# A 31-tap causal convolution summed in a PSUM bank, by halves of the tokens

## The chip, the cores and the metric

The kernel runs on one core of a Trainium2 chip. The metric is the device time of one execution in microseconds (us); a difference is told from the median of several runs. The engines are named as in the profile: PE is TensorE with its matmuls (PEld its weight loads), DVE is VectorE, ACT is ScalarE, POOL is GpSimd, and SP is the engine that issues the transfers. SBUF is the working memory, PSUM the memory that matmuls write: eight banks, each of which holds 512 float32 columns on every partition.

## The reference

One layer of a decoder over 1024 tokens of width 1024, batch 1. A normed and modulated input `h` is projected once; the columns go to four token mixers, whose outputs are joined and projected again, and a gated feed-forward block follows.

```
h = rmsnorm(x, ln1_g) * (1 + sc1) + sh1
a_val, a_gate, b_q, b_k, b_v, b_g, b_lr, c_q, c_k, c_v, d_u, d_v = split(h @ w_in)
o_a = silu(layernorm(causal_dwconv(a_val * sigmoid(a_gate), conv_w, conv_b)))   # CONV_K = 31, 256 channels
o_b = gla_mixer(b_q, b_k, b_v, b_g, b_lr, ...)      # gates from b_lr @ gla_w2
o_c = dilated_attention(c_q, c_k, c_v, cos, sin)    # rotary, masked scores, softmax
o_d = sgu_mixer(d_u, d_v, ...)
x = x + g1 * (concat(o_a, o_b, o_c, o_d) @ w_out)
x = x + g2 * conv_ffn(rmsnorm(x, ln2_g) * (1 + sc2) + sh2, ...)
out = rmsnorm(x, lnf_g)
```

The causal convolution works on each of the 256 channels by itself: y[s] = bias + the sum over j = 0..30 of w[30 - j] * h[s - j], with zeros ahead of the first token.

## The kernel before

The convolution has its channels on partitions and the tokens in columns: two tiles (`t` = 0, 1) of 128 channels and 1024 tokens. `hA[t]` holds the gated input, `yA[t]` the sum, both in SBUF. The generator `conv_taps` issues one DVE operation for each tap: L461 multiplies by the last weight and adds the bias, and L464 runs 30 times over the rest, each of which adds a shifted product to `yA[t]` in place: it reads `hA[t]` and `yA[t]` in SBUF and writes `yA[t]`. That makes 62 operations of nearly 1024 columns.

The rest of the mixers is woven around it. Every part of the work is a generator. `weave` runs a main one (projections on PE) and after each of its steps takes as many steps from the others as their rate allows; `conv` has the rate 2.74, 1.87 and 1.39 taps a step in the three stages that it spans. A framework then fixes the order on every engine, allots the buffers of its pools and adds the waits. Each engine works through its own queue strictly in order.

```
    weave(chain(proj_feat(gate1, (1,))), (conv, 2.74))
    weave(chain(proj_feat(rope("q0")), proj_feat(rope("k0")), proj_tok(c_v), proj_feat(rope("q1")), proj_feat(rope("k1"))),
          (conv, 1.87))
```

The names that the prediction uses: `p_s()` gives one of eight PSUM banks (tile `s_ps`), which the projections, scores and transposes share. Four gates (L454 sigmoid on ACT, L456 product on DVE) make `hA`. The projections of the attention (q0, k0, c_v, q1, k1) end in copies on ACT (L593 for q and k); for q and k four transfers on SP then swap halves of 32 partitions (L597, L598), and POOL does the rotation in three operations (L601 to L603). Weights are split into two parts, a cast on ACT (L70) and a difference on POOL (L71). In the next stage the projection `proj_glr` runs over eight token tiles; of each result DVE copies 16 columns into `lrs` (L752), and PE transposes them (L755). Beside it the attention starts: PE's scores (L92 to L94, `m_t,x_t`), DVE's masked maximum (L659, which reads the mask that L631 loads), ACT's exponential (L667), the quotient on DVE (L670), POOL (L672) and ACT, and transposes on PE (L695). L828 is a matmul of the modulation, which DVE adds up (L830).

Of the kernel before, what the change touches and what calls it, by code (L numbers as in the profile page):

```python
# [7 lines left out]
F32 = mybir.dt.float32  # L8
# [3 lines left out]
ALU = mybir.AluOpType  # L12
AX = mybir.AxisListType

P = 128
D = 1024
S = 1024
KT = D // P
# [3 lines left out]
CONV_K = 31  # L22
# [3 lines left out]

# feature tiles of the first modulation, in the order of their loads
ADA_1 = ((0,), (1,), (2, 3), (4, 5), (6, 7))

# first columns of the parts of w_in  # L30
C_AV, C_AG = 0, 256
# [5 lines left out]

# columns of the packed per-feature vectors
O_C, O_L1, O_L2, O_CG, O_CB, O_VB, O_GB, O_SB, O_AB = 0, 8, 16, 24, 26, 28, 30, 31, 35
O_CW = 83  # L40
# [6 lines left out]
def trunk(ctx, tc, x, cols, ada_1, ada_2, ada_b, w_a, w_feat, w_tok, w_glr, gla_w2, gla_norm_g,  # L47
# [3 lines left out]
    ve, ac, gp, pe, sy = nc.vector, nc.scalar, nc.gpsimd, nc.tensor, nc.sync  # L51


    cst = ctx.enter_context(tc.tile_pool(name="cst", bufs=1))
# [18 lines left out]
    def rsqrt(dst, ss, shape, scale, pool):  # L73
        # bit-level first guess, three Newton steps
        v = pool.tile(shape, F32, tag="rs_v", name="rs_v", bufs=2)
        t = pool.tile(shape, F32, tag="rs_t", name="rs_t", bufs=2)
        ve.tensor_scalar(v, ss, scale, EPS, op0=ALU.mult, op1=ALU.add)
        ve.tensor_scalar(dst.bitcast(I32), v.bitcast(I32), -0.5, 1597463007.0, op0=ALU.mult, op1=ALU.add)
        for _ in range(3):
            ve.tensor_tensor(t, dst, dst, op=ALU.mult)  # L80
            ve.scalar_tensor_tensor(t, t, -0.5, v, op0=ALU.mult, op1=ALU.mult)
            ve.scalar_tensor_tensor(dst, t, 1.5, dst, op0=ALU.add, op1=ALU.mult)
# [15 lines left out]

    # ---------------------------------------------------------------- constants
    ident = cst.tile([P, P], F32, name="ident")  # L100
# [6 lines left out]
    def cc(o, n=1):  # L107
        return col[:, o:o + n]
# [4 lines left out]
    adab1 = cst.tile([P, 2, KT], F32, name="adab1")  # L113
    mod = cst.tile([P, 5, KT], F32, name="mod")      # scale and shift of the first norm, of the second norm, gate of the feed-forward block

    # ---------------------------------------------------------------- emission: streams woven into one order
    active = []
# [9 lines left out]
    def weave(main, *bgs):  # L127
        credit = [0.0] * len(bgs)
        for _ in main:
            for n, (g, rate) in enumerate(bgs):  # L130
                credit[n] += rate
                while credit[n] >= 1:
                    credit[n] -= 1
                    next(g, 0)
            step()
# [8 lines left out]
    class Weights:  # L144
        """Weight tiles in the order of their use: loaded two ahead, split one ahead."""

# [33 lines left out]

    # ---------------------------------------------------------------- mixers
    ph1 = ExitStack()
# [8 lines left out]
    def p_s():  # L191
        return ps1.tile([P, 512], F32, tag="s", name="s_ps", bufs=8)
# [3 lines left out]

    # first norm: statistics, transposes
    g1b = c1.tile([P, 1024], F32, name="g1b")
# [3 lines left out]
    PM = (4, 0, 0, 0, 0)  # L202
# [12 lines left out]

    # the first PM[p] products of a group on TensorE, the others on VectorE
    def ada_mac(p):
# [70 lines left out]

    # modulation of the first norm and the first projections, feature tile by feature tile
    hH = [[None, None] for _ in range(KT)]  # L290
# [88 lines left out]

    # ---------------------------------------------------------------- projections  # L380
    def proj_feat(done, halves=(0, 1)):
        wh, wl = W1.get()
        for g in halves:
            ps = p_s()
            for k in range(KT):
                ks = slice(k * P, (k + 1) * P)
                mm3(ps, wh[:, ks], wl[:, ks], hH[k][g], hL[k][g], k == 0, k == KT - 1)
                if k == 3:
                    yield 1
            if g == 1:  # L390
                spawn(W1.refill())
            spawn(done(g, ps))
            yield 1
# [46 lines left out]
    def chain(*gens):  # L440
        for g in gens:
            yield from g

    have = set()                                     # what of oT is there, by (tile, half of the tokens)
    oT = [None] * 8                                  # feature-major outputs of the mixers, by tiles of 128 features
    oH = [[None, None] for _ in range(8)]
    oL = [[None, None] for _ in range(8)]

    # ---------------------------------------------------------------- A: gate, convolution, norm
    hA = [t_m(), t_m()]  # L450
# [7 lines left out]
    def conv_taps():  # L458
        for t in range(2):
            y = yA[t]  # L460
            ve.tensor_scalar(y, hA[t], cc(O_CW + 60 + t), cc(O_VB + t), op0=ALU.mult, op1=ALU.add)  # L461
            yield 1
            for s in range(1, CONV_K):
                ve.scalar_tensor_tensor(y[:, s:], hA[t][:, :S - s], cc(O_CW + (CONV_K - 1 - s) * 2 + t), y[:, s:], op0=ALU.mult, op1=ALU.add)  # L464
                yield 1

    def conv_norm():
# [44 lines left out]

    # ---------------------------------------------------------------- D: spatial gating
    dk = t_m()
# [63 lines left out]

    # ---------------------------------------------------------------- C: rotary
    cosT, sinT = t_m(), t_m()  # L580
# [35 lines left out]

    # first stage: the rest of A's and all of D's and C's projections, the convolution beside them
    conv = conv_taps()

    def gate1(g, ps):  # L620
# [3 lines left out]
    step()  # L624
    weave(chain(proj_feat(gate1, (1,))), (conv, 2.74))
    weave(chain(proj_feat(rope("q0")), proj_feat(rope("k0")), proj_tok(c_v), proj_feat(rope("q1")), proj_feat(rope("k1"))),
          (conv, 1.87))

    # ---------------------------------------------------------------- C: attention
    maskT = t_m()  # L630
# [87 lines left out]

    # ---------------------------------------------------------------- B: gates
    ngb = c1.tile([P, 64], F32, name="ngb")  # L720
# [83 lines left out]

    # ---------------------------------------------------------------- modulation of the rest
    ada_flat = ada_b.rearrange("a b -> (a b)")
# [42 lines left out]

    # second stage: B's projections, attention beside them  # L850
    att = attention([(hp, qb) for hp in range(2) for qb in range(NT)])
    weave(chain(proj_glr(), proj_tok(b_v), proj_feat(b_q), proj_feat(b_k)), (conv, 1.39), (att, 0.83), (ada, 2.06))
    flush(conv)
    cn = conv_norm()

    # ---------------------------------------------------------------- B: gated linear attention
    def split_o(kt, g):
# [107 lines left out]

    # third stage: D's projections, the rest of the attention and the linear attention beside them
    def delay(n, g):
# [17 lines left out]

    # ---------------------------------------------------------------- output projection, second norm, by halves of the tokens
    x1 = [None] * NT
# [77 lines left out]

    # ---------------------------------------------------------------- feed-forward block
    ph2 = ctx.enter_context(tc.tile_pool(name="ph2", bufs=1, reuse_waits="tile"))
# [94 lines left out]

    # last norm, by token tiles
    rows = {}

    def final(i, nh):
        if nh == 0:
            rows[i] = t_y(), ph2.tile([P, 4], F32, tag="ssf", name="ssf", bufs=2)
        t, ss = rows[i]
        cs = half(nh)  # L1170
        ac.activation(t[:, cs], x1[i][:, cs], AF.Square, accum_out=ss[:, 0:1])  # L1171
        ve.tensor_scalar(ss[:, nh + 1:nh + 2], ss[:, 0:1], 1.0 / D, ss[:, 1:2] if nh else EPS, op0=ALU.mult, op1=ALU.add)  # L1172
        gp.tensor_tensor(x1[i][:, cs], x1[i][:, cs], lnf[:, cs], op=ALU.mult)
        if nh == 1:
            # each Newton step multiplies by -2 (and the powers of it that the last one left), which lnf takes back
            v, w, u = ss[:, 2:3], rr[:, i:i + 1], ss[:, 3:4]
            ve.tensor_scalar(w.bitcast(I32), v.bitcast(I32), -0.5, 1597463007.0, op0=ALU.mult, op1=ALU.add)  # L1177
            for c in (1.0, -2.0, 16.0):
                ve.scalar_tensor_tensor(u, w, v, w, op0=ALU.mult, op1=ALU.mult)  # L1179
                ve.scalar_tensor_tensor(w, u, 3.0 * c * c, w, op0=ALU.subtract, op1=ALU.mult)  # L1180
            ac.mul(t[:, half(1)], x1[i][:, half(1)], w)  # L1181
            ve.tensor_scalar(t[:, half(0)], x1[i][:, half(0)], w, None, op0=ALU.mult)  # L1182
            sy.dma_start(out[i * P:(i + 1) * P, :], t)
# [86 lines left out]
```

## Time and profile before

| what | value |
|---|---|
| median of 3 runs | 1289.31 us (1288.96 to 1294.81) |
| span of the profiled execution, first to last instruction | 1287.0 us |
| median of the runs less that span | 2.3 us |
| busy: PE, DVE, POOL, ACT | 94%, 58%, 38%, 30% of the span |
| mean granted clock of PE | 0.978 |

The page gives the profiled execution by its span; its whole time is not listed apart from the runs, so the span is set beside their median. The mixers take the first 540 us or so, the feed-forward block the rest. Busy shares are means over all stages: where an engine matters is read from stretches of the span and from what each engine waits for.

### The profile page before, as it was taken

How to read it: one execution, taken by the hardware profiler on the slowest of the kernel's cores; microseconds unless marked ns; L12 is line 12 of the kernel's file. 1: busy time of each engine (PE TensorE's matmuls, PEld its weight loads, DVE VectorE, ACT ScalarE, POOL GpSimd, SP SyncE). 2: the span in 40 equal slices, each digit the busy share in tenths (PEclk: the TensorE clock that was granted, in tenths of full speed). 3: DMA queues.
4: the chain of work that ended last, by engine and by line, in shares of the span. 5: the costliest groups of instructions: out<-in, count | busy, mean ns of one | idle time of the engine just before them, and what ended most of it. 6: DMA issues, size and time to landing. Idle time of an engine off the chain costs nothing. (4 is left out here: it accounts for less than half of the span.)

```text
span 1287.0 us, 15986 instructions
## 1 busy us (share of the span) xinstructions
PE 1206.2 (94%) x6466; PEld 1013.9 (79%) x6466; DVE 746.1 (58%) x1193; ACT 390.8 (30%) x553; POOL 486.1 (38%) x260
## 2 busy tenths in 40 slices
PE   5899928999998999999999999999999999999995
PEld 4679817866797899978888888888888888888884
DVE  6989999576697965463534342425343434343467
ACT  5541205464331523343131313131212121212323
POOL 2557833322232466655141414131323232322424
PEclk9999968999998999999999999999999999999998
DMA  8632310222332532302020212121202021212102
GB/s 322 241 109 68 94 40 21 71 79 78 99 108 71 197 110 83 115 19 86 28 80 19 67 33 66 33 66 33 66 33 66 33 66 33 66 33 62 36 17 115
DMA packets 32842, 98.50 MB, mean 77 GB/s; under 512 B 3952, under 2 KB 5120, under 8 KB 32768
## 3 DMA queue, kind: packets, MB, share of 16 engines
q1 hardware_dynamic: 32768, 97.48, 23.3%
q8 instruction: 51, 0.84, 0.3%
q14 instruction: 23, 0.19, 0.0%
HBM read 91.17 MB, written 4.19 MB: 74 GB/s over the span
## 5 line engine op out<-in xcount | busy, mean ns | idle before, releaser
L71 POOL TENSOR_TENSOR wh_t<-wf_t,wh_t 128x1024 fp32r<-128x1024 f32 (+1 forms) x79 | 196.9, 2494 | 305.0 <-ACT wh_t L70 296.3
L92 PE MATMUL z_ps<-h_t,wh_t 128*128 128x512 f32 x704 | 274.4, 390 | 0.7 <-DVE y_t L1089 0.7
L93 PE MATMUL z_ps<-h_t,wh_t 128*128 128x512 f32 x704 | 274.8, 390 | 0.2 <-POOL h_t L71 0.2
L94 PE MATMUL z_ps<-h_t,wh_t 128*128 128x512 f32 x704 | 274.4, 390 | 0.0
L1089 DVE SCALAR_TENSOR_TENSOR y_t<-z_ps,col,y_t 128x1023 f32<-128x1023 f32 x88 | 112.5, 1280 | 227.8 <-ACT y_t L1086 226.7
L1157 DVE TENSOR_TENSOR x_t<-d_ps,x_t 128x512 f32<-128x512 f32 x170 | 116.7, 688 | 165.7 <-PE d_ps L94 165.7
L70 ACT CAST wh_t<-wf_t 128x1024 fp32r<-128x1024 f32 (+1 forms) x81 | 85.1, 1050 | 296.5 <-PE z_ps L92 136.9
L92 PEld LDWEIGHTS z_ps<-h_t,wh_t 128*128 128x128 f32 x704 | 132.2, 188 | 28.8 <-POOL wh_t L71 0.8
L93 PEld LDWEIGHTS z_ps<-h_t,wh_t 128*128 128x128 f32 x704 | 132.2, 188 | 28.5 <-POOL h_t L71 0.6
L94 PEld LDWEIGHTS z_ps<-h_t,wh_t 128*128 128x128 f32 x704 | 132.2, 188 | 27.4
L94 PE MATMUL d_ps<-wd_t,p_t 128*128 128x512 f32 x320 | 125.5, 393 | 0.0
L92 PE MATMUL d_ps<-wd_t,p_t 128*128 128x512 f32 x320 | 125.2, 391 | 0.0
L93 PE MATMUL d_ps<-wd_t,p_t 128*128 128x512 f32 x320 | 125.0, 391 | 0.0
L464 DVE SCALAR_TENSOR_TENSOR m_t<-m_t,col 128x1023 f32<-128x1023 f32 (+29 forms) x60 | 116.3, 1939 | 1.7
L71 POOL TENSOR_TENSOR wd_t<-wf_t,wd_t 128x1024 fp32r<-128x1024 f32 x20 | 47.7, 2403 | 160.2 <-ACT wd_t L70 160.2
L92 PE MATMUL s_ps<-wh_t,h_t 128*128 128x256 f32 (+1 forms) x320 | 93.7, 296 | 0.0
L93 PE MATMUL s_ps<-wh_t,h_t 128*128 128x256 f32 (+1 forms) x320 | 91.7, 287 | 0.9 <-POOL wh_t L71 0.9
L94 PE MATMUL s_ps<-wh_t,h_t 128*128 128x256 f32 (+1 forms) x320 | 91.7, 287 | 0.0
L1140 POOL TENSOR_TENSOR wf_t<-wf_t,g2b 128x1024 f32<-128x1024 f32 x22 | 53.9, 2449 | 77.1 <-DMA wf_t<-in_ffn_down 76.4
L821 DVE SCALAR_TENSOR_TENSOR acc<-ad,cond,acc 128x256 f32<-128x256 f32 x112 | 74.1, 665 | 12.4 <-DMA ad<-in_ada 10.5
L93 PEld LDWEIGHTS d_ps<-wd_t,p_t 128*128 128x128 f32 x320 | 60.2, 188 | 13.4
L92 PEld LDWEIGHTS d_ps<-wd_t,p_t 128*128 128x128 f32 x320 | 60.1, 188 | 13.3
(252 smaller groups left out, 2115.8 us busy)
## 6 DMA issues: line engine op xcount, KB each, us to landing
wf_t<-in_ffn_up SPq DMA_DIRECT2D x44, 512.0 KB, 3.6
ad<-in_ada SPq DMA_DIRECT2D x64, 256.0 KB, 3.4
wf_t<-in_ffn_down SPq DMA_DIRECT2D x22, 512.0 KB, 3.6
x_t<-in_x SPq DMA_DIRECT2D x16, 512.0 KB, 6.3
wf_t<-in_w_out SPq DMA_DIRECT2D x16, 512.0 KB, 3.7
m_t<-in_ada SPq DMA_DIRECT2D x12, 512.0 KB, 9.5
wf_t<-in_w_tok SPq DMA_DIRECT2D x8, 512.0 KB, 3.6
out<-y_t SPq DMA_DIRECT2D x8, 512.0 KB, 2.6
```

What stands on the lines that cost most here:

```text
L70: ac.copy(dst_h, src)
L71: eng.tensor_tensor(dst_l, src, dst_h.bitcast(F32), op=ALU.subtract)
L92: pe.matmul(ps, ll, rh, start=first, stop=False)
L93: pe.matmul(ps, lh, rl, start=False, stop=False)
L94: return pe.matmul(ps, lh, rh, start=False, stop=last)
L464: ve.scalar_tensor_tensor(y[:, s:], hA[t][:, :S - s], cc(O_CW + (CONV_K - 1 - s) * 2 + t), y[:, s:], op0=ALU.mult, op1=ALU.add)
L821: ve.scalar_tensor_tensor(acc, f[:, kk, :], cond[:, k:k + 1], acc, op0=ALU.mult, op1=ALU.add)
L1089: ve.scalar_tensor_tensor(y[:, s:e], z[:, s - n:e - n], cc(O_FW + 88 - 44 * n + f), y[:, s:e], op0=ALU.mult, op1=ALU.add)
L1140: gp.tensor_tensor(w[:, :1024], w[:, :1024], g2b, op=ALU.mult)
L1157: ve.tensor_tensor(x1[i][:, cs], pd, x1[i][:, cs], op=ALU.add)
```

## The change

`conv_taps` goes through each tile in two halves of 512 tokens. A half gets a PSUM bank `y` from `p_s()`. The first operation writes the last weight's product and the bias into it, and the next 29 add to it in place; they read `hA[t]` in SBUF and `y` in PSUM and write `y`. The last tap reads `y` and writes its half of `yA[t]` in SBUF. The first half has no input for the first `s` tokens of tap `s`, so it works on columns `s` to 511, and the last tap's 30 first columns go to `yA[t]` by a copy on ACT (L469). That makes 124 operations of up to 512 columns and two copies; the rates at which they are woven in are about doubled. Comments are also taken out, which moves nothing.

```
     def conv_taps():
         for t in range(2):
-            y = yA[t]
-            ve.tensor_scalar(y, hA[t], cc(O_CW + 60 + t), cc(O_VB + t), op0=ALU.mult, op1=ALU.add)
-            yield 1
-            for s in range(1, CONV_K):
-                ve.scalar_tensor_tensor(y[:, s:], hA[t][:, :S - s], cc(O_CW + (CONV_K - 1 - s) * 2 + t), y[:, s:], op0=ALU.mult, op1=ALU.add)
+            h = hA[t]
+            for g in range(2):
+                y, o, e = p_s(), 512 * g, 512 * g + 512
+                ve.tensor_scalar(y, h[:, o:e], cc(O_CW + 60 + t), cc(O_VB + t), op0=ALU.mult, op1=ALU.add)
                 yield 1
+                for s in range(1, CONV_K):
+                    a = 0 if g else s
+                    last = s == CONV_K - 1
+                    if last and a:
+                        ac.copy(yA[t][:, o:o + a], y[:, :a])
+                    ve.scalar_tensor_tensor(yA[t][:, o + a:e] if last else y[:, a:], h[:, o + a - s:e - s],
+                                            cc(O_CW + (CONV_K - 1 - s) * 2 + t), y[:, a:], op0=ALU.mult, op1=ALU.add)
+                    yield 1
...
-    weave(chain(proj_feat(gate1, (1,))), (conv, 2.74))
+    weave(chain(proj_feat(gate1, (1,))), (conv, 3.9))
     weave(chain(proj_feat(rope("q0")), proj_feat(rope("k0")), proj_tok(c_v), proj_feat(rope("q1")), proj_feat(rope("k1"))),
-          (conv, 1.87))
+          (conv, 3.8))
...
-    weave(chain(proj_glr(), proj_tok(b_v), proj_feat(b_q), proj_feat(b_k)), (conv, 1.39), (att, 0.83), (ada, 2.06))
+    weave(chain(proj_glr(), proj_tok(b_v), proj_feat(b_q), proj_feat(b_k)), (conv, 2.8), (att, 0.83), (ada, 2.06))
```

In the changed kernel the taps are L470 and each line behind them has a number higher by 7 (L752 is L759 there, L659 is L666). The text uses the numbers of before for all that both kernels have. PE's and POOL's orders are the same in both, apart from these numbers.

DVE, around the first `lrs`. `s_ps` and `m_t` with `col` are the convolution, `mx` is the score's maximum, and the brackets name the engines that a row waits for. Before, 55 operations of the convolution stand ahead of the first `lrs`:

```order
L464 SCALAR_TENSOR_TENSOR m_t<-m_t,col 128x1004 [waits DVE_49]
L659 ISA m_t,mx<-s_ps,m_t 128x128 [waits DMAHW3_49,DMAHW4_49,DMAHW2_49,DMAHW5_49,PE_49,DMAHW6_49,Activation_49,Pool_49]
L659 ISA mx 128x1
L464 SCALAR_TENSOR_TENSOR m_t<-m_t,col 128x1003 [waits DVE_49]
L663 TENSOR_SCALAR mx<-mx 128x1 [waits DVE_49]
L464 SCALAR_TENSOR_TENSOR m_t<-m_t,col 128x1002 [waits DVE_49]
L830 TENSOR_TENSOR g1b<-s_ps,adb 128x256 [waits PE_49]
L670 RECIPROCAL den<-den 128x1 [waits Activation_49]
L464 SCALAR_TENSOR_TENSOR m_t<-m_t,col 128x1001 [waits DVE_49]
L752 COPY lrs<-s_ps 128x16 [waits Activation_49]
```

In the changed kernel the same place has 108 halves ahead of it, and the first of these rows is the last tap of the first half of tile 1, which waits for ACT's copy:

```order
L470 SCALAR_TENSOR_TENSOR m_t<-m_t,col,s_ps 128x482 [waits Activation_49,Pool_49]
L470 SCALAR_TENSOR_TENSOR s_ps<-m_t,col,s_ps 128x512 [waits DVE_49] x4
L837 TENSOR_TENSOR g1b<-s_ps,adb 128x256 [waits DMAHW2_49,PE_49]
L470 SCALAR_TENSOR_TENSOR s_ps<-m_t,col,s_ps 128x512 [waits DVE_49]
L666 ISA m_t,mx<-s_ps,m_t 128x128 [waits DMAHW4_49,DMAHW3_49,DMAHW5_49,DMAHW2_49,Pool_49]
L666 ISA mx 128x1
L470 SCALAR_TENSOR_TENSOR s_ps<-m_t,col,s_ps 128x512 [waits DVE_49]
L759 COPY lrs<-s_ps 128x16 [waits Activation_49]
```

Ahead of `lrs` stand the same kinds of work, with L830 now ahead of L659 and L670 behind `lrs`. 16 halves are left behind the first `lrs`, where 7 taps were.

ACT, where the first rotary results are copied (`m_t<-s_ps` of 512 columns is such a copy). The changed kernel's order has the new copy of 30 columns between two of them, behind the cast of the rotated q0, which waits for POOL:

```order
L70 CAST m_t<-x_t 128x1024 [waits DMAHW6_49,DMAHW5_49,DMAHW7_49,DMAHW0_49,Pool_49]
L600 COPY m_t<-s_ps 128x512
L469 COPY m_t<-s_ps 128x30 [waits DVE_49]
L600 COPY m_t<-s_ps 128x512 [waits PE_49]
L70 CAST wh_t<-wf_t 128x1024 [waits DMAHW1_49,PE_49,Activation_49]
```

Before, the two copies follow each other directly. The second L469, of tile 1, stands behind the last of these copies (k1) and ahead of the copies of `proj_glr`.

SP, at the swaps of k1 (`x_t<-m_t`) and the load of the mask (`in_dil_mask`). Before:

```order
L154 DMA wf_t<-in_w_tok 128x1024 [waits DMAHW7_49,DMAHW5_49,Pool_49]
L631 DMA m_t<-in_dil_mask 128x1024
L597 DMA x_t<-m_t 32x1024 [waits Activation_49]
L598 DMA x_t<-m_t 32x1024 [waits DMAHW0_49]
L597 DMA x_t<-m_t 32x1024 [waits DMAHW1_49]
L598 DMA x_t<-m_t 32x1024 [waits DMAHW2_49]
```

In the changed kernel:

```order
L154 DMA wf_t<-in_w_tok 128x1024 [waits DMAHW7_49,DMAHW5_49,Pool_49]
L604 DMA x_t<-m_t 32x1024 [waits Activation_49]
L605 DMA x_t<-m_t 32x1024
L604 DMA x_t<-m_t 32x1024 [waits DMAHW0_49]
L605 DMA x_t<-m_t 32x1024 [waits DMAHW1_49]
L638 DMA m_t<-in_dil_mask 128x1024 [waits DMAHW2_49]
```

The mask has moved behind the four swaps, the first of which waits for ACT's copy of k1.

## Rows read from the trace of the kernel before

**Rows 1.** The page: busy time by engine, and the group of the taps.

```profile
PE 1206.2 (94%) x6466; PEld 1013.9 (79%) x6466; DVE 746.1 (58%) x1193; ACT 390.8 (30%) x553; POOL 486.1 (38%) x260
...
L464 DVE SCALAR_TENSOR_TENSOR m_t<-m_t,col 128x1023 f32<-128x1023 f32 (+29 forms) x60 | 116.3, 1939 | 1.7
```

**Rows 2.** What PE waited for: in total, times, longest.

```profile
PE s_ps L755 <- DVE lrs L752: 30.3, 1, 30.3
```

**Rows 3.** Stretches of 5 us: PE, PEld, DVE, ACT, POOL busy, clock, DMA.

```profile
170.00:175.00 5.00, 0.00 (x0) 0.00 (x0) 4.89 (x4) 0.00 (x0) 0.94 (x1) 0.63 0.00 0
...
200.00:205.00 5.00, 5.00 (x24) 4.78 (x23) 5.00 (x10) 0.00 (x0) 2.48 (x1) 0.50 0.00 0
205.00:210.00 5.00, 5.00 (x40) 4.29 (x38) 5.00 (x16) 4.20 (x9) 1.17 (x2) 0.96 0.00 0
```

**Rows 4.** Timeline of PE: start, length, instruction, and idle time before it.

```profile
140.63 0.39 PE L92 MATMUL s_ps<-h_t,wh_t 128*128 128x512 f32 x1
...
162.87 0.59 PE L828 MATMUL s_ps<-acc,ones 128*128 128x256 f32 x2
164.39 0.39 PE L93 MATMUL s_ps<-wh_t,h_t 128*128 128x272 f32 x1 [0.92 <-POOL wh_t L71]
...
199.07 0.38 PE L755 MATMUL s_ps<-ident,lrs 128*16 128x128 f32 x1 [30.28 <-DVE lrs L752]
...
205.71 0.27 PE L755 MATMUL s_ps<-ident,lrs 128*16 128x128 f32 x1
...
209.78 0.27 PE L755 MATMUL s_ps<-ident,lrs 128*16 128x128 f32 x1
```

**Rows 5.** Timeline of DVE, equal instructions merged.

```profile
92.35 66.85 DVE L464 SCALAR_TENSOR_TENSOR m_t<-m_t,col 128x1020 f32<-128x1020 f32 x27
...
162.01 32.25 DVE L464 SCALAR_TENSOR_TENSOR m_t<-m_t,col 128x1023 f32<-128x1023 f32 x20
194.18 0.28 DVE L659 CUSTOM_DVE_ANT_0 m_t<-s_ps,m_t 128x128 f32<-128x128 f32 x1
...
198.85 0.17 DVE L752 COPY lrs<-s_ps 128x16 f32<-128x16 f32 x1
```

**Rows 6.** Two stretches, all engines; then L464 from 105 to 140 (min/median/max).

```profile
106.00:136.00 30.00, 30.00 (x224) 28.80 (x223) 29.65 (x11) 4.12 (x5) 28.26 (x9) 1.00 0.27 74
...
171.00:194.00 23.00, 0.00 (x0) 0.00 (x0) 22.40 (x18) 0.00 (x0) 0.00 (x0) 0.51 0.00 0
...
L464 DVE SCALAR_TENSOR_TENSOR m_t<-m_t,col x13: 1264/3285/3298, 102.8 to 138.7; 128x1013 f32<-128x1013 f32 x1, 128x1012 f32<-128x1012 f32 x1, 128x1011 f32<-128x1011 f32 x1, 128x1010 f32<-128x1010 f32 x1
```

**Rows 7.** Timeline of POOL: q0's rotation begins; a split beside no tap.

```profile
106.89 2.77 POOL L601 TENSOR_TENSOR x_t<-x_t,m_t 128x1024 f32<-128x1024 f32 x1 [1.86 <-DMA x_t<-m_t]
...
224.00 2.37 POOL L71 TENSOR_TENSOR wh_t<-wf_t,wh_t 128x1024 fp32r<-128x1024 f32 x1 [3.84 <-ACT wh_t L70]
```

**Rows 8.** DVE operations on PSUM: two lines (ns min/median/max), then groups by form.

```profile
L1089 DVE SCALAR_TENSOR_TENSOR y_t<-z_ps,col,y_t x88: 1269/1282/1285, 568.8 to 1231.9; 128x1023 f32<-128x1023 f32 x44, 128x1022 f32<-128x1022 f32 x44
...
L1157 DVE TENSOR_TENSOR x_t<-d_ps,x_t x170: 673/691/692, 617.9 to 1278.5; 128x512 f32<-128x512 f32 x170
...
L1044 DVE TENSOR_SCALAR hf<-s_ps,mod 128x512 f32<-128x512 f32 x8 | 6.4, 806 | 3.6 <-PE s_ps L263 3.6
...
L791 DVE SCALAR_TENSOR_TENSOR m_t<-s_ps,m_t 128x512 f32<-128x512 f32 x2 | 1.4, 680 | 0.0
...
L335 DVE MEMSET s_ps<- 128x512 f32 x1 | 0.5, 485 | 1.0 <-PEq L1260 1.0
```

**Rows 9.** SP's and ACT's timelines, and the mask's time to landing.

```profile
150.65 0.44 SPq L631 DMA_DIRECT2D m_t<-in_dil_mask  x1
...
160.18 0.59 SPq L598 DMA_DIRECT2D x_t<-m_t  x1
...
157.75 0.58 ACT L593 COPY m_t<-s_ps 128x512 f32<-128x512 f32 x1
...
DMA to landing us min/median/max: 4.4/4.4/4.4
```

## The prediction

> **What bounds the kernel now.** I read the page first: PE is busy for 94% of the span, and the taps (L464, on DVE) are 60 instructions of 1939 ns in the mean [rows 1]. A PE-bound kernel gains from a faster DVE only where PE waits for DVE, so the list of PE's waits came next. It has one large entry: 30.3 us, once, for `lrs` of L752 on DVE [rows 2]. In stretches of 5 us that is a PE that does nothing from 170 to 175 while DVE is busy for 4.89 of them, and that comes back with a granted clock of 0.50, the lower of its two levels, and has it until about 205 [rows 3]. PE's timeline has the wait as a single row: L755 at 199.07 after 30.28 us of idling, so PE had its work done at 168.8 [rows 4].
>
> What is late there? L752 copies 16 columns, 0.17 us, but stands in DVE's order behind 55 operations of the convolution. DVE works on them without a gap: 27 taps in 66.85 us, then the end of tile 0, then 20 taps in 32.25 us; the first score maximum (L659, 194.18) and L752 (198.85) follow with no idle time noted ahead of them [rows 5]. So DVE's queue is the cause, and nothing that DVE itself waits for.
>
> And why 1.9 us for a tap? Where POOL is nearly always at work (106 to 136: 28.26 of 30 us), 11 taps take 29.65 us; where it is idle (171 to 194), 18 take 22.40 us, 1.24 us each [rows 6]. A tap alone takes 1264 ns or little more, and the median between 105 and 140 is 3285 [rows 6]; POOL's nine operations take 28.26 / 9 = 3.1 us in the mean, and 2.37 where DVE does not run taps beside one [rows 6, 7]. Both engines lose to each other. Of 60 taps some (116.3 - 60 x 1.27) / 2.03 = 20 are stretched.
>
> **The change, part by part.** *The price of a half.* The trace before has no operation that reads SBUF and PSUM and writes PSUM. The nearest row is L791: the same operation over 512 columns with one input in PSUM and one in SBUF, 680 ns [rows 8]. Bounds: 485 ns for the only DVE write into PSUM over 512 columns (L335, reads nothing) and 806 ns for the dearest PSUM reader over 512 (L1044) [rows 8]. Unstretched taps follow each other every 1.244 us and are about 1.27 long, so I take 0.03 off for the overlap: 0.65 us from start to start.
>
> *The stretch.* L1089 and L1157 are the two operations before with just one input in SBUF that run for long beside POOL: 88 of the first lie between 1269 and 1285 ns, 170 of the second between 673 and 692, no stretched one among them [rows 8]. A half also has one SBUF input. I take it as never stretched: 124 x 0.65 = 81 us of DVE for all of the convolution, where L464 alone took 116.3.
>
> [...]
>
> *When `lrs` is ready.* PE's and POOL's orders do not change. In DVE's, 108 halves stand ahead of L752 where 55 whole operations did. Ten come before the last gate (L456), which waits for PE and is done at 92.35 as before, when the next tap starts [rows 5]. The next 31 end at 92.35 + 31 x 0.65 = 112.5. Then comes a new wait: the last tap of tile 0's first half waits for ACT's copy of 30 columns (L469), which stands behind the cast of the first rotary result, so behind three POOL operations that start at 106.89 [rows 7]: 106.89 + 3 x 2.4 + 1.9 for ACT's cast and two copies (one of 512 columns is 0.58 [rows 9]) = 116.0. DVE idles 3.5 us, which hides in its new slack. Queued behind L469 on ACT are the next rotary copy and a weight cast; the tap that L469 needs is done by 112, so it is not late for them. From 116.0 another 60 halves end at 155.0, where tile 1's L469 is waited for: behind ACT's L593 of 157.75, so 158.6 [rows 9]. Five halves more: 161.9. L830 then waits for PE's L828 (ends 163.46 [rows 4]), as before.
>
> L659 needs the mask, and SP's queue is changed just there: the mask's transfer went out at 150.65, now it stands behind the four swaps, the last at 160.18. So issued at 160.8, it lands 4.4 us later, 165.2 [rows 9]. L659 (0.3), one half (0.65) and L752 put `lrs` at 166.3. PE wants it at 168.8, or 0.9 sooner (below): no wait. The cover is 1.6 us; without it (a half at over 0.73 us) each further 0.1 us costs 6.5 us.
>
> *Banks.* The sums hold two of the eight banks at a time. PE's second half of the q1 projection, begun at 140.63 [rows 4], now waits for the bank that the tap at 116 frees, and the first score, just ahead of L828, for one freed at 116 + 39 x 0.65 = 141. Both cost nothing, with over 20 us of cover each.
>
> *The sum.* Out go: the wait, 30.28. The slow clock behind it: from L755 at 199.07 to the next at 205.71 PE takes 6.64 us, the next such step 4.07 with larger scores [rows 4]; 2.6 to 3.3, I take 2.9. The wait at 164.39 for POOL's L71, 0.92 [rows 4], because POOL gets through its rotary work some 0.8 us an operation faster. Together 34.1. Against that 1.0, between 0 and 5, for small waits behind it: DVE was busy nearly all of 200 to 210 [rows 3], and the same 16 remaining halves (10.4 us, before 7 taps) now stand in a stretch that PE crosses faster. Net 33.1: the span goes from 1287.0 to 1253.9. The median of the runs is 2.3 us above the profiled span, so the time is 1289.3 - 33.1 = **1256 us**.
>
> **The rivals.** *One half for one POOL operation (slower).* If halves did contend, DVE and POOL would take turns as now, one for one: 20 turns of 2.4 + 0.65 = 3.05 us where they were 3.3, but with half the work done in each. 20 halves x 0.65 = 13 us would be left over, less 20 x 0.25 = 5 saved in the turns: `lrs` 8 us later than 198.85 and the time 1297. (With the excess of each POOL operation unchanged and only the fixed cost added, 124 x 0.65 - 62 x 1.244 = 3.5 us, it would be 1293.) For it: whole taps do behave so. Against: 258 operations without one stretched. It decides if halves between 106 and 136 last over 1.0 us. 5%.
>
> *The halves are dear.* At 0.80, near the upper row, `lrs` comes at 116 + 65 x 0.80 + 4 = 172, 4 us late: 1260; at 0.90 1267. For it: writes to PSUM with two reads are not in the trace. Against: L791. 12%.
>
> *The wait moves on.* Each later step of the chain (scores, maximum, exponential on ACT, L672 on POOL, transposes on PE) has a wait for another engine; before, the 30 us let all of them catch up. If DVE or ACT runs behind PE for the eight `lrs` steps, 6 to 14 us come back: 1261 to 1269. For it: DVE 5.00 of 5 us busy at 200 to 210. Against: the steps behind 205.71 already run at full clock with no large wait. 15%.
>
> *No gain.* If the wait was for something else that L659 needs (mask, POOL), it stays: 1286 to 1292. Against: no idle time on DVE ahead of it [rows 5]. 4%.
>
> **How the numbers follow.** The forecast as worked out, 1251 to 1261, has 64%; the rivals 5, 12, 15 and 4. The range 1249 to 1268 holds the forecast and most of the dear halves and of the moved wait, leaving out the two rivals without gain and the tails, under 2 in 10. A difference of under 0.5% (6.4 us) is about what cannot be told from none here. Faster 0.91, same 0.04, slower 0.05.
>
> **What would show it.** Right: L470 at 0.6 to 0.75 us in the mean with no row over 1 us; no wait of PE for L752's successor over 2 us; granted clock 1.00 from 165 to 205; POOL's rotary operations at 2.4 us; `lrs` copied before 168. Wrong: a half over 0.73 us from start to start, halves of 2 to 3 us beside POOL, PE waits of several us on transposes or scores between 170 and 215, or the mask landing after 167.

## The result, and the profile after

The changed kernel takes 1257.07 us, median of 4 runs (1254.72 to 1259.65), the kernel before 1290.47 us in the same comparison (4 runs, 1288.96 to 1294.81): ratio 0.974, 95% interval 0.9709 to 0.9771. It is faster by 33 us, against a forecast of 1256 us. The profiled execution spans 1256.5 us (before 1287.0) at a mean granted clock of 0.989 (0.978).

First the page of the changed kernel, busy time by engine and the group of the halves, which answers to [rows 1]:

```profile
PE 1205.3 (96%) x6466; PEld 1013.1 (81%) x6466; DVE 708.5 (56%) x1255; ACT 391.4 (31%) x555; POOL 465.4 (37%) x260
...
L470 DVE SCALAR_TENSOR_TENSOR s_ps<-m_t,col,s_ps 128x512 f32<-128x512 f32 (+19 forms) x116 | 80.4, 743 | 1.1
```

PE works as long as before (1205 us), in a span that is 30.5 us shorter. DVE and POOL have shed 37.6 and 20.7 us of busy time, though DVE has more instructions. What PE waited for, the longest entries (total, times, longest), beside [rows 2]:

```profile
PE s_ps L303 <- DMA m_t<-in_ada: 10.9, 1, 10.9
PE s_ps L330 <- ACT h_t L317: 6.9, 2, 3.6
PE s_ps L303 <- DVE acc L223: 3.5, 2, 3.2
...
PE s_ps L92 <- DVE g1b L837: 1.1, 1, 1.1
```

The wait of 30.3 us for `lrs` is not in the list at all, and no new one of its kind has come. DVE's timeline (start, length, merged instructions, idle time before and its releaser) shows why, against [rows 5]:

```profile
92.20 9.26 DVE L470 SCALAR_TENSOR_TENSOR s_ps<-m_t,col,s_ps 128x502 f32<-128x502 f32 x12
...
115.73 0.72 DVE L470 SCALAR_TENSOR_TENSOR m_t<-m_t,col,s_ps 128x482 f32<-128x482 f32 x1 [1.66 <-ACT m_t L469]
...
118.53 22.32 DVE L470 SCALAR_TENSOR_TENSOR s_ps<-m_t,col,s_ps 128x512 f32<-128x512 f32 x34
...
158.37 0.72 DVE L470 SCALAR_TENSOR_TENSOR m_t<-m_t,col,s_ps 128x482 f32<-128x482 f32 x1 [2.88 <-ACT m_t L469]
...
165.64 0.29 DVE L666 CUSTOM_DVE_ANT_0 m_t<-s_ps,m_t 128x128 f32<-128x128 f32 x1 [1.20 <-issue]
...
166.51 0.17 DVE L759 COPY lrs<-s_ps 128x16 f32<-128x16 f32 x1
```

From 118.53 to the next tap at 140.75 there are 34 halves in 22.22 us, 0.654 us each, in a stretch in which POOL is busy for 14.5 us. `lrs` is copied at 166.51 instead of 198.85. The halves as one line (min/median/max) and POOL's first rotary operations, against [rows 6, 7]:

```profile
L470 DVE SCALAR_TENSOR_TENSOR s_ps<-m_t,col,s_ps x116: 721/747/757, 82.8 to 182.9; 128x512 f32<-128x512 f32 x58, 128x511 f32<-128x511 f32 x2, 128x510 f32<-128x510 f32 x2, 128x509 f32<-128x509 f32 x2
```

```profile
L608 POOL TENSOR_TENSOR x_t<-x_t,m_t x4: 2397/2402/2412, 106.7 to 163.4; 128x1024 f32<-128x1024 f32 x4
```

No half is stretched, though 78 of the 120 taps have a POOL operation beside them, and POOL's operation takes 2.40 us where it took 2.6 to 3.4. PE's timeline around the places that gave and took time, and its windows (PE, PEld, DVE, ACT, POOL busy, clock, DMA), against [rows 3, 4]:

```profile
167.30 0.28 PE L762 MATMUL s_ps<-ident,lrs 128*16 128x128 f32 x1
...
182.55 0.39 PE L92 MATMUL s_ps<-wh_t,h_t 128*128 128x272 f32 x1 [1.06 <-DVE g1b L837]
...
194.56 0.39 PE L92 MATMUL s_ps<-m_t,x_t 64*128 64x256 f32 x1 [0.31 <-DVE pt L708]
```

```profile
170.00:175.00 5.00, 5.00 (x41) 4.53 (x40) 5.00 (x18) 3.66 (x8) 2.24 (x2) 1.00 0.00 0
...
265.00:270.00 5.00, 4.17 (x13) 2.08 (x12) 3.96 (x21) 2.59 (x8) 0.00 (x0) 0.71 0.31 105
270.00:275.00 5.00, 5.00 (x15) 3.89 (x15) 1.57 (x4) 1.46 (x3) 1.37 (x1) 0.61 0.01 3
```

PE's order is the same in both kernels, so one subtraction tells where the time went: how much earlier the same PE instruction starts than before.

| PE instruction (before, after) | earlier by | what happened since the row above |
|---|---|---|
| 61.13, 61.02 | 0.1 us | |
| 164.39, 162.97 | 1.4 | no wait for POOL's L71 |
| 199.07, 167.30 | 31.8 | no wait for `lrs` |
| 205.47, 170.94 | 34.5 | no stretch at the lower clock (before 0.50 at 200 to 205, here 1.00) |
| 215.74, 182.55 | 33.2 | wait for L837 |
| 227.29, 194.56 | 32.7 | wait for L708 |
| 296.60, 263.84 | 32.8 | |
| 303.51, 273.94 | 29.6 | a stretch at the lower clock, 265 to 275 (0.71, 0.61; before 1.00) |
| 403.13, 370.48 | 32.7 | before has such a stretch at 395 to 405 (clock 0.66) |
| 541.71, 511.28 | 30.4 | small waits, and one stretch at 395 to 400 (0.68) |

### The profile page after: what moved, and what is told of

Read it like the earlier page. It is cut to its first block, busy times and chain, and to the rows that moved or that the text cites. A ratio compares the mean times of both kernels' runs of the same rounds, so it can differ in the third digit from the quotient of the medians.

```text
span 1256.5 us, 16045 instructions
## 1 busy us (share of the span) xinstructions
PE 1205.3 (96%) x6466; PEld 1013.1 (81%) x6466; DVE 708.5 (56%) x1255; ACT 391.4 (31%) x555; POOL 465.4 (37%) x260
## 5 line engine op out<-in xcount | busy, mean ns | idle before, releaser
L71 POOL TENSOR_TENSOR wh_t<-wf_t,wh_t 128x1024 fp32r<-128x1024 f32 (+1 forms) x79 | 192.3, 2435 | 315.5 <-ACT wh_t L70 302.1
L1096 DVE SCALAR_TENSOR_TENSOR y_t<-z_ps,col,y_t 128x1023 f32<-128x1023 f32 x88 | 112.5, 1280 | 225.7 <-ACT y_t L1093 224.5
L1164 DVE TENSOR_TENSOR x_t<-d_ps,x_t 128x512 f32<-128x512 f32 x170 | 116.6, 688 | 165.6 <-PE d_ps L94 165.6
L92 PEld LDWEIGHTS z_ps<-h_t,wh_t 128*128 128x128 f32 x704 | 132.2, 188 | 29.6 <-POOL wh_t L71 0.8
L71 POOL TENSOR_TENSOR wd_t<-wf_t,wd_t 128x1024 fp32r<-128x1024 f32 x20 | 47.7, 2403 | 160.1 <-ACT wd_t L70 160.1
L470 DVE SCALAR_TENSOR_TENSOR s_ps<-m_t,col,s_ps 128x512 f32<-128x512 f32 (+19 forms) x116 | 80.4, 743 | 1.1
L828 DVE SCALAR_TENSOR_TENSOR acc<-ad,cond,acc 128x256 f32<-128x256 f32 x112 | 71.7, 644 | 14.5 <-DMA ad<-in_ada 12.8
L93 PEld LDWEIGHTS d_ps<-wd_t,p_t 128*128 128x128 f32 x320 | 60.3, 188 | 13.3
L70 ACT CAST wd_t<-wf_t 128x1024 fp32r<-128x1024 f32 x20 | 20.1, 1046 | 163.3 <-PE d_ps L93 161.7
```

The costliest lines, as they stand in the source:

```text
L70: ac.copy(dst_h, src)
L71: eng.tensor_tensor(dst_l, src, dst_h.bitcast(F32), op=ALU.subtract)
L92: pe.matmul(ps, ll, rh, start=first, stop=False)
L93: pe.matmul(ps, lh, rl, start=False, stop=False)
L470: ve.scalar_tensor_tensor(yA[t][:, o + a:e] if last else y[:, a:], h[:, o + a - s:e - s], cc(O_CW + (CONV_K - 1 - s) * 2 + t), y[:, a:], o ...
L828: ve.scalar_tensor_tensor(acc, f[:, kk, :], cond[:, k:k + 1], acc, op0=ALU.mult, op1=ALU.add)
```

## The experiments

The changed kernel and the ten of the experiments are each compared with the kernel before on the same chip. The DVE column is the time in which DVE is busy with taps, overlaps counted once, over both groups where a kernel has two (changed: 80.4 in PSUM, and four last taps of 2.9 in all; e4: 60.5 + 41.8 + 2 x 0.73).

| kernel | median us | ratio (95%) | taps on DVE, us | `lrs` at | PE waits for it |
|---|---|---|---|---|---|
| before | 1290.1 to 1290.5 | 1 | 116.3 | 198.9 | 30.3 |
| changed | 1257.07 | 0.974 (0.971 to 0.977) | 83.3 | 166.5 | 0 |
| e2, POOL light | 1266.69 | 0.983 (0.980 to 0.986) | 93.7 | 177.4 | 10.2 |
| e1, halves in SBUF | 1294.77 | 1.003 (1.002 to 1.005) | 118.3 | 204.3 | 3.5 |
| e7, the same in one chain | 1305.1 | 1.011 (1.008 to 1.014) | 134.5 | 203.5 | 36.3 |
| e3, input in PSUM | 1254.59 | 0.973 (0.970 to 0.976) | 78.5 | 165.2 | 0 |
| e4, tile 1 in SBUF | 1273.89 | 0.988 (0.985 to 0.990) | 104 | 180.9 | 11.9 |
| e9, whole taps alternating | 1294.52 | 1.003 (1.001 to 1.005) | 114.2 | 203.8 | 34.0 |
| e5, middle rate 0.5 | 1286.86 | 0.997 (0.995 to 0.998) | 112.7 | 166.0 | 0 |
| e10, middle rate 1.2 | 1287.45 | 0.998 (0.996 to 1.000) | 119.1 | 179.9 | 12.0 |
| e6, copies and mask moved | 1257.14 | 0.973 (0.970 to 0.975) | 82.9 | 165.6 | 0 |
| e8, quarters | 1266.23 | 0.980 (0.977 to 0.982) | 99.6 | 163.8 | 0 |

**Is POOL the cause? (e2)** Whole taps in SBUF as before, without most of POOL's rotary work.

```
+            r = slice(0, 16)
-            gp.tensor_tensor(Y, Y, sinT, op=ALU.mult)
+            gp.tensor_tensor(Y[:, r], Y[:, r], sinT[:, r], op=ALU.mult)
...
```

> The kernel before, whole taps in SBUF, with the twelve rotary operations of POOL on 16 columns of 1024 (the rotation of the other columns is left out). Theory (a tap is long because POOL works beside it, 2.03 us for each POOL operation of full length): 12 x 2.03 = 24 us less for the taps (some 92 us in all instead of 116), lrs at about 175, PE's wait for it about 6 us, the slow clock behind it shorter, 1263 us (1258 to 1268). Rival (taps are long for another reason, as the transfers of the swaps or PE's own traffic): the taps keep 110 us or more, the wait 25 us or more, 1283 us or more.

The group of the taps and PE's wait:

```profile
L464 DVE SCALAR_TENSOR_TENSOR m_t<-m_t,col 128x1023 f32<-128x1023 f32 (+29 forms) x60 | 93.7, 1568 | 1.6
```

```profile
PE s_ps L756 <- DVE lrs L753: 10.2, 1, 10.2
```

The taps lose 22.6 us with no edit on DVE at all, and 9 of the 60 are stretched where 20 were. Each POOL operation of full length costs the taps 22.6 / 12 = 1.9 us (2.03 had been worked out). The time, 1267, lies in the range, the wait 4 us above what was written, since `lrs` came at 177.4 and not 175 and PE was ready for it at 167.4 and not at 168.8.

**Is it the halving, or PSUM? (e1)** The changed kernel with the sum back in SBUF.

```
-                y, o, e = p_s(), 512 * g, 512 * g + 512
+                o, e = 512 * g, 512 * g + 512
+                y = yA[t][:, o:e]
...
-                    last = s == CONV_K - 1
-                    if last and a:
-                        ac.copy(yA[t][:, o:o + a], y[:, :a])
```

> The changed kernel with the sum of each half back in SBUF, in place: halves and rates of the change, but two inputs in SBUF. PE's order is that of both kernels; DVE has 112 halves ahead of the first lrs. Theory (two SBUF inputs make a tap share with POOL): halves alone take 0.60 to 0.65 us, those beside a POOL operation 2 to 3.1 us, POOL's rotary operations about 3 us; lrs comes at 195 to 207, PE waits 27 to 38 us for it, and the time is 1286 to 1299 us. Rival (the gain comes from the finer grain, the order or the rates, not from PSUM): no half over 1 us, no wait of PE for lrs over 2 us, 1254 to 1260 us.

The time falls in the theory's range, but not by the theory's way. PE's longest waits, then three rows of POOL:

```profile
PE s_ps L410 <- POOL wh_t L71: 16.6, 1, 16.6
PE s_ps L93 <- POOL wh_t L71: 11.2, 2, 10.6
...
PE s_ps L760 <- DVE lrs L757: 3.5, 1, 3.5
```

```profile
101.95 26.80 POOL L71 TENSOR_TENSOR wh_t<-wf_t,wh_t 128x1024 fp32r<-128x1024 f32 x1 [7.89 <-ACT wh_t L70]
128.71 2.82 POOL L606 TENSOR_TENSOR x_t<-x_t,m_t 128x1024 f32<-128x1024 f32 x1
...
166.30 20.72 POOL L71 TENSOR_TENSOR wh_t<-wf_t,wh_t 128x1088 fp32r<-128x1088 f32 x1 [5.11 <-ACT wh_t L70]
```

Most halves (102 of 120) run at 0.74 us as if they were alone, and POOL's weight split, 2.37 us where no tap runs beside it [rows 7], stands still beside them for 26.8 and 20.7 us. PE then waits 27.2 us for POOL's weights in place of 30.3 for `lrs`. The rival (the finer grain brings the gain) falls: halves in SBUF gain nothing (1294.77 us). That POOL is kept out was in neither theory. In DVE's order the two halves of a tile alternate here, as two independent chains, and the long POOL operation ends when that does: the alternating halves of tile 0 end at about 125.9 (43 halves of 0.65 us from 97.76), POOL's split 2.9 us later. The second one ends at 187.0, 2.3 us after DVE has nothing left to start: from 184.7 it waits 9.33 us for the mask, which is part of why `lrs` is late here. The next experiment takes the alternation away.

**Short operations in one chain (e7).**

```
-                o, e = 512 * g, 512 * g + 512
+                o, e = 511 * g, 512 * g + 512
```

> Halves with the sum in SBUF, as in the first experiment, but the second half of a tile starts a column earlier, so that it can only begin when the first is done: one chain of dependent operations instead of two that alternate (for some 8 pairs at the change of tiles two chains still alternate). Theory (POOL was kept out for 26.8 and 20.7 us because DVE's operations alternated between independent chains): POOL's operations take 2.4 to 3 us, but for one that may start where chains alternate (up to 11 us); halves beside POOL take about 2.8 us; lrs comes at 190 to 198, PE waits 20 to 28 us for it, little for POOL's weights; 1282 to 1292 us. Rival (short operations keep POOL out in any order): POOL operations of 15 us and more, PE waits for L71 of 8 us and more, no long wait for lrs, 1290 to 1300 us.

POOL's row at 109, the halves from 104 to 118 (min/median/max), and PE's wait:

```profile
109.05 2.82 POOL L607 TENSOR_TENSOR m_t<-m_t 128x1024 f32<-128x1024 f32 x1
```

```profile
L468 DVE SCALAR_TENSOR_TENSOR m_t<-m_t,col x7: 732/2747/2752, 102.6 to 115.2; 128x494 f32<-128x494 f32 x1, 128x493 f32<-128x493 f32 x1, 128x492 f32<-128x492 f32 x1, 128x491 f32<-128x491 f32 x1
```

```profile
PE s_ps L760 <- DVE lrs L757: 36.3, 1, 36.3
```

POOL is no longer kept out (2.8 us), and a half beside it lasts 2.75 us: one half for one POOL operation, the first rival of the prediction made real, and the time is above that of any whole tap kernel: 1305 us. What was expected of POOL and of the halves holds. The time was put too low by 13 us at its upper end. `lrs` came at 203.5 and not by 198, but only 4.7 us of what this kernel loses to the one before are there when PE gets it. Another 12 go between 219 and 305, where PE's order also differs in part from that of before, and 2 come back; so 1305 us is not the price of the turns alone.

**One input in SBUF, or the sum in PSUM? (e3)** The operands change places: the input stands in a bank, the sum in SBUF.

```
+    def load_h(t, g):
+        h = p_s()
+        ac.copy(h, hA[t][:, 482 * g:482 * g + 512])
+        hp.append(h)
...
+                h, y, o = hp.pop(), yA[t][:, 512 * g:512 * g + 512], 30 * g
...
+                    ve.scalar_tensor_tensor(y[:, a:e], h[:, o + a - s:o + e - s], cc(O_CW + (CONV_K - 1 - s) * 2 + t), y[:, a:e], op0=ALU.mult, op1=ALU.add)
```

> The changed kernel with the operands' places exchanged: the input of each half is copied into a PSUM bank by ACT, and the sum stays in SBUF, in place, so that a half reads one input in PSUM and one in SBUF and writes SBUF. The last 30 tokens of each tile get only their first product (left out). Theory (what counts is one input in SBUF, not where the sum is written): halves of 0.65 to 0.75 us, none over 1 us, POOL's rotary operations 2.4 us, no wait of PE for lrs over 2 us, 1254 to 1261 us. Rival (a sum that is read and written in SBUF contends too; only the PSUM sum escapes): halves of 2 to 3 us beside POOL, a wait of over 20 us, 1280 us or more.

The halves as one line (min/median/max):

```profile
L474 DVE SCALAR_TENSOR_TENSOR m_t<-s_ps,col,m_t x120: 699/711/750, 82.5 to 177.9; 128x482 f32<-128x482 f32 x62, 128x511 f32<-128x511 f32 x2, 128x510 f32<-128x510 f32 x2, 128x509 f32<-128x509 f32 x2
```

None of 120 halves is stretched (77 have a POOL operation beside them), and the time is that of the changed kernel (the intervals overlap nearly wholly). In these runs the sum may be written to SBUF; what counted was that one of the two tensor inputs is in PSUM: 0.75 us at most here, 2.75 beside POOL in e7 with both in SBUF.

**Half a dose (e4).** Tile 0 as changed, tile 1 as before.

```
             h = hA[t]
+            if t == 1:
+                y = yA[t]
+                ve.tensor_scalar(y, h, cc(O_CW + 60 + t), cc(O_VB + t), op0=ALU.mult, op1=ALU.add)
...
+                return
```

> The changed kernel with tile 1 as before (31 whole taps in SBUF), tile 0 in halves in PSUM; PE's order unchanged. Theory (each POOL operation of full length costs a whole tap beside it 2.0 us, and lrs is late by the sum): tile 1 starts at about 128, about 8 POOL operations run beside its first 23 taps, 16 us, of which some 3 go into waits that DVE has there anyway: lrs 11 to 15 us later than in the changed kernel, PE waits 10 to 14 us, some 2 us of slow clock, 1271 us (1266 to 1276). Rivals: the gain needs only a few taps less (1254 to 1260), or it needs all of them in PSUM (1285 or more).

PE's longest wait (total, times, longest):

```profile
PE s_ps L772 <- DVE lrs L769: 11.9, 1, 11.9
```

`lrs` is 14.4 us later than in the changed kernel (180.91 against 166.51), the wait 11.9, the time 16.8 more: all within what the theory wrote, and neither of the two rivals.

**Does the order alone do it? (e5, e10)** The kernel before, with another rate of the middle stage and no other edit.

```
-          (conv, 1.87))
+          (conv, 0.5))
```

> The kernel before, whole taps in SBUF, with the rate of the middle stage at 0.5 instead of 1.87, so that 31 operations of the convolution (tile 0) stand ahead of the first lrs on DVE and not 55; all of tile 1 comes behind the eighth lrs. Theory (the wait is DVE's queue ahead of lrs, whatever fills it): tile 0 is done by 145, lrs before 168, no wait of PE for it over 2 us; tile 1's 31 taps then cost 40 to 50 us of DVE later, with waits of some 0 to 12 us: 1256 to 1270 us. Rival (only a tap that does not share with POOL brings the gain; the contention costs the same wherever the taps stand): 1280 us or more.

The wait for `lrs` goes, as expected, and PE is 33.6 us ahead at 205. But that is given back by 304, and the expectation's 1256 to 1270 us is wrong. The time is the rival's, 1280 or more, and the taps cost what they did: 112.7 us, 19 of 60 stretched. PE's largest new wait, and a window of 20 us (PE, PEld, DVE, ACT, POOL busy, clock, DMA):

```profile
PE s_ps L833 <- DVE acc L821: 12.8, 2, 7.1
```

```profile
255.00:275.00 20.00, 12.91 (x65) 8.51 (x64) 19.00 (x34) 8.51 (x15) 1.22 (x1) 0.50 0.01 3
```

The 30 taps of tile 1 now stand between 224.9 and 294.7 among the attention's own DVE work, DVE is busy for 19.0 of 20 us, and PE, idle for a third of them, runs at the lower clock (0.50). In e10 the rate was 1.2:

> The kernel before, whole taps in SBUF, with the middle stage's rate at 1.2 instead of 1.87: 41 operations of the convolution ahead of the first lrs instead of 55, and 8 behind the last of the eight. Theory (DVE has too much work up to about 300 us, so that an order only moves the wait): lrs at 175 to 182, PE waits 7 to 14 us for it, and further waits of 5 to 20 us come behind it; 1276 to 1290 us. Rival (a middle order gains as much as the change, since nothing behind 215 is late): 1256 to 1270 us.

As the theory wrote, 12.0 us of the wait stay, and 9.2 come at L828 and 3.7 at L833, both for DVE's sums (L821). PE's waits:

```profile
PE s_ps L755 <- DVE lrs L752: 12.0, 1, 12.0
...
PE s_ps L828 <- DVE acc L821: 9.2, 1, 9.2
```

So both of these orders move the wait, and what removed it here was less DVE work. (PE's order is that of before up to 262 in e5 and up to 219 in e10, and differs in part from there to about 300.) "The queue ahead of `lrs`" was where the excess showed, not all that it was.

**Do alternating chains keep POOL out by themselves? (e9)** Whole taps, with tile 1 running 12 taps behind tile 0.

```
+        for n in range(CONV_K + 12):
+            for t, s in ((0, n), (1, n - 12)):
...
```

> The kernel before, whole taps in SBUF, with tile 1 started 12 taps behind tile 0, so that DVE's operations alternate between two independent chains from about 97 us on for 24 pairs. Orders of PE and POOL unchanged. Theory (POOL is kept out as long as DVE's operations follow each other from independent chains): the POOL operation that starts at about 102 lasts until the pairs end, at 150 to 160; taps meanwhile take 1.25 us; PE waits 35 to 50 us for POOL's weights and little for lrs; 1295 to 1340 us. Rival (only short operations keep POOL out): POOL operations of 2.4 to 3.5 us, taps beside them of 3.3 us, no wait of PE for L71 over 2 us, but a longer one for lrs than before (61 taps ahead instead of 55): 1290 to 1302 us.

POOL's timeline, the operation that starts at about 102 and the next:

```profile
102.96 3.14 POOL L71 TENSOR_TENSOR wh_t<-wf_t,wh_t 128x1024 fp32r<-128x1024 f32 x1 [8.31 <-ACT wh_t L70]
107.68 2.93 POOL L604 TENSOR_TENSOR x_t<-x_t,m_t 128x1024 f32<-128x1024 f32 x1 [1.59 <-DMA x_t<-m_t]
```

POOL gets its turns (2.48 to 3.45 us each between 100 and 172, a tap up to 3.53), and PE's wait is again for `lrs` (34.0 us); the theory that the alternation alone keeps POOL out falls. In these runs it took both, short operations and independent chains (26.80 us in e1).

**Do the new waits cost anything? (e6)** The copies on DVE, the mask's load ahead of the middle stage.

```
-                        ac.copy(yA[t][:, o:o + a], y[:, :a])
+                        ve.tensor_copy(yA[t][:, o:o + a], y[:, :a])
...
+    maskT = t_m()
+    sy.dma_start(maskT, dil_mask)
     conv = conv_taps()
```

> The changed kernel with the two copies of 30 columns on DVE instead of ACT, and the mask loaded ahead of the middle stage. Theory (the waits of 1.66 and 2.88 us for those copies and the 1.20 us for the mask lie in DVE's slack): they go, lrs comes 2 to 5 us earlier, PE's timeline up to 182 is the same within 0.5 us, and the time is 1254 to 1259 us, the same. Rival (DVE's waits there still set the end): 1253 us or less.

The waits for L469 are gone, and the first score maximum starts at 161.15 and not at 165.64, but after 5.60 us in which DVE idles; `lrs` comes 0.9 us earlier (165.6) and not 2 to 5, and the median is the same, 1257.14. The waits lay in slack. Its profiled execution is shorter, 1250.7 us: PE no longer waits 1.06 us at L837, and there is no lower clock from 265 to 275 (1.00). With the medians equal, that is not shown to last over the runs.

**What does an operation cost by itself? (e8)**

```
-            for g in range(2):
-                y, o, e = p_s(), 512 * g, 512 * g + 512
+            for g in range(4):
+                y, o, e = p_s()[:, :256], 256 * g, 256 * g + 256
```

> The changed kernel in quarters: 248 operations of up to 256 columns, each quarter in a bank of its own, rates doubled again. DVE has 186 of them ahead of the first lrs. Theory (each operation has a fixed part: two halves cost 1.31 us where a tap alone takes 1.244): a quarter takes 0.35 to 0.40 us from start to start, the convolution 87 to 99 us of DVE instead of 81; none is stretched by POOL; lrs by 170, and the 62 quarters left behind it (16 halves before) make PE wait some us more between 165 and 215: 1257 to 1266 us. Rival (no fixed part that matters): 0.33 us, 1254 to 1259 us.

DVE's timeline, 35 quarters in a row, and the first score maximum:

```profile
119.67 13.73 DVE L470 SCALAR_TENSOR_TENSOR s_ps<-m_t,col,s_ps 128x256 f32<-128x256 f32 x35
...
170.31 0.29 DVE L666 CUSTOM_DVE_ANT_0 m_t<-s_ps,m_t 128x128 f32<-128x128 f32 x1 [4.21 <-DMA m_t<-in_dil_mask]
```

35 quarters take 13.63 us up to the next operation at 133.30, 0.389 us each, none stretched. With 0.654 for a half, 256 columns cost 0.265 and an operation 0.389 - 0.265 = 0.12 us by itself, an estimate from these two numbers, where operations of different banks alternate. The expectation's 1.244 us for a tap alone is too low: from start to start it is 1.31 (see the price of a half, below). The time does not measure that alone: the order moved the mask's load to 162.02, and DVE waited 4.21 us for it, PE 1.84 behind it.

## Why the prediction was right, step by step

**The cause.** That whole taps are long because POOL and they hold each other up, and that a half in PSUM is free of it, is shown: less POOL work shortens the taps (e2: 93.7 us for 116.3), halves without PSUM gain nothing (e1: 1294.77 us, e7: 1305.1), either operand in PSUM does as well (e3: 1254.59 against 1257.07), and half a dose gives half the effect (e4: 1273.89). With one input in SBUF no half is stretched, of 116 in the changed kernel (757 ns at most) and 120 in e3 (750). How the turns go matters too, as e1 (26.80 us for one POOL operation) and e7 (2.82 us, and 2.75 for a half beside it) show.

**The price of a half.** Forecast 0.65 us from start to start; measured 0.654 where halves of two banks alternate, as from 118.53 on. Where halves of one bank follow each other, as the 12 from 92.20, it is 0.775. Of the steps from one half straight to the next, 67 take 0.63 to 0.66 us and 30 take 0.77 to 0.79. The prediction did not know this difference, and its working for 0.65 is wrong in two places. The rows' length, 743 ns in the mean, is above the 680 ns of L791. And taps of one chain do not overlap, as DVE's timeline of before shows:

```profile
172.06 22.21 DVE L464 SCALAR_TENSOR_TENSOR m_t<-m_t,col 128x1020 f32<-128x1020 f32 x17
```

These 17 taps, each about 1.27 us long, start every 1.31 us. The 22.40 us of [rows 6] are DVE's busy time in 23 us, over 16 whole taps and parts of two, so 1.244 is no step from one tap to the next. Alternating halves do overlap, by 0.743 - 0.654 = 0.09 us, and that cancels the other error. So the price is right partly by luck: it hangs on an order in which two banks alternate. (The whole taps of e9's two chains start every 1.16 to 1.20 us where POOL is not at work.) Two alternating halves, 1.31 us, cost DVE as much as one whole tap of a chain; the 124 x 0.65 - 62 x 1.244 = 3.5 us that the prediction works out for the cost of halving are not there. The 30 dear steps are above the 0.73 that was written as a sign of being wrong. They came, but the rival of dear halves did not: the first 31 halves behind the last gate end at 114.07 and not at 112.5, the next 60 take 39.8 us and not 39, and DVE's idle time before L469's taps took that up.

**When `lrs` is ready.** Forecast 166.3, measured 166.51, by the steps that were written. The copies and the mask's load as they ran:

```profile
115.45 0.19 ACT L469 COPY m_t<-s_ps 128x30 f32<-128x30 f32 x1
...
158.09 0.18 ACT L469 COPY m_t<-s_ps 128x30 f32<-128x30 f32 x1
```

```profile
160.66 1.46 SPq L638 DMA_DIRECT2D m_t<-in_dil_mask  x1
```

The taps that wait for L469 start at 115.73 and 158.37 (forecast 116.0 and 158.6), after 1.66 and 2.88 us of idle time (forecast 3.5 and 3.6). The mask is issued at 160.66 (160.8). PE starts L762 at 167.30 without a wait. The cover was thus under 0.8 us, not 1.6: PE was there 1.4 us earlier than before, where the text had allowed 0.9, and `lrs` 0.2 us later than forecast. In e8 the mask is what ran late.

**The banks.** PE's timeline is the same within 0.3 us from 85 to 163, so neither of the two waits for a bank cost anything.

**The sum.** The wait was put at 30.28 and measured 31.77 - 1.42 = 30.35. The slow clock, forecast 2.9, measured 34.53 - 31.77 = 2.76. POOL's wait, forecast 0.92, measured 1.42 at the same instruction, 0.15 of which PE was ahead before it. Together 34.5 against 34.1. The term that was mis-sized is the one for small waits behind: 1.0 was taken, and from 34.5 to the 30.5 us by which the spans differ it is 4.0, inside its bounds of 0 to 5. Small waits at 182 and 194 make 1.8. The lower clock between 265 and 275 (0.71, 0.61) in this execution takes 3.2 (32.76 to 29.57), but the kernel before loses 3.1 in such a stretch of its own, at 395 to 405 (0.66). The last 2.2 go in a stretch at the lower clock from 395 to 400 (0.68) and in small waits up to 511. So the span is 1256.5 and not 1253.9. That the time still came within 1.1 us is partly luck: the median lies 0.6 us above the profiled span, where 2.3 had been allowed. The profiled execution, 1258.28 us, is 1.2 us slower than the median; the medians differ by 33.4 us, near the 33.1 worked out, and the profiled spans by 30.5.

**The rivals.** One half for one POOL operation does happen when the sum is in SBUF in one chain (e7). A turn took 2.8 us there where 3.05 had been worked out, and `lrs` came 4.7 us later than before, not 8; the time, 1305, is above the 1297 worked out by what PE loses behind it. The moved wait came for some 2 us. That DVE at 5.00 of 5 us busy would hold PE up proved true only in part: DVE is as busy from 170 to 175 (5.00 of 5 us), and PE does not wait there (5.00).

## What to carry to other kernels

When one kind of instruction has two lengths, find the engine that is busy only beside the long ones, count the long ones, and price the excess (20 x 2.03 us here); it is worth removing where the engine that it delays stands ahead of one that is the bound. Work that was only moved out of the way was paid for later here, where DVE was nearly full (19.0 of 20 us in e5): both slower rates removed most of the wait for `lrs` (all of 30.3 us, and 18.3) and gained 3 us. And cutting operations small is not harmless in itself: halves with two inputs in SBUF lost 5 and 15 us (of the 15, 5 up to `lrs`), and gained 33 with one. With one input in PSUM, operations of independent sums had better alternate: a half behind its own predecessor cost 0.12 us more here (0.775 against 0.654).

## What was not expected of the hardware

In e1 DVE kept POOL out: one POOL operation, of 2.37 us where no tap runs, lasted 26.80 us, another 20.72, beside halves of 0.74 us with two SBUF inputs whose chains alternate. In one chain, halves and POOL take turns at 2.75 us (e7); whole taps take turns in one chain (3.29 us, the median between 105 and 140 before) and in two (up to 3.53 us, e9). In e1 there are also turns, from 126 to 162, where POOL's operations follow each other closely, with alternating halves from 143 on (two in 3.56 us); both long ones started after POOL had been idle for over 5 us (7.89 and 5.11). Why a newly started POOL operation is shut out there, and not beside whole taps, stays open.
